# A one-core decoder layer: the queues of every engine but TensorE in another order, with each step naming its buffers

## The chip, the cores and the metric

One Trainium2 chip, one core. The metric is device microseconds of one execution of the whole kernel; lower is better. Engines are written as in the profile: PE (TensorE; PEld is its weight load), DVE (VectorE), ACT (ScalarE), POOL (GpSimd) and SP (SyncE, which here does nothing but issue DMAs).

## The reference, cut to what matters

The layer is computed in float32 on 512 positions of 1024 channels (depth 1).

```python
h   = rms_norm(x, attn_pre_norm)
mix = hybrid_mixer(h, ...)            # two head groups, one input and one output projection
x   = x + rms_norm(mix, attn_post_norm)
h   = rms_norm(x, ffn_pre_norm)
f   = (silu(h @ w_gate) * (h @ w_up)) @ w_down      # 1024 -> 2816 -> 1024
out = x + rms_norm(f, ffn_post_norm)
```

`hybrid_mixer` projects h, rotates queries and keys, and runs differential attention (4 heads: softmax of one map minus lambda times softmax of a second, values of 128) and native sparse attention (8 heads in 2 groups, with a compressed, a selected and a window branch, mixed by sigmoid gates). Both results are concatenated and multiplied by `w_out`.

## The kernel before

**Precision.** Every factor of a matmul is cut into a high part (ACT copies the float32 tile to fp32r) and a low part (DVE subtracts the high part from the tile), and a product is three matmuls: high by high, high by low, low by high. So nearly every weight tile costs one transfer, one ACT instruction and one DVE instruction of 512 or 1024 columns.

**The order is written by hand.** The kernel defines some 2600 named steps, each a function that issues a handful of instructions, and then calls them in the order of two long strings: `PLAN` (1387 steps: projection, attention, output projection) and `PLAN_NORM` with `PLAN_END` (1198 steps: norms and feed-forward). Nothing reorders behind that. Each engine takes its own instructions in the order in which the steps were called, and waits for data or a buffer where it must. So the place of a step among the steps of the same engine is that engine's queue, and the place among steps of other engines matters only through tiles: a tile is granted when its step is called. `at(t, fn, ...)` also notes a time for each step of the second half (`todo`), which orders only steps that stand in neither string.

**Stages.** To about 90 us the input projection runs: `xL`/`xH`/`xl` load and cut the eight tiles of x, `bL`/`bh`/`bl` and `fL`/`fh`/`fl` the weights, `F6.0` and the like are the matmuls. Up to about 230 us come the heads, `D0` to `D3` and `N0` to `N7`: `S` scores on PE, `X` the row maximum on DVE (L1051), `E` the exponential on ACT (L1055), `M` scaling on POOL (L1224), `T` transposes on PE, `H` and `L` the high and low parts (L1082 on ACT, L1085 on DVE), `V` the product with the values. `D0OH` is the high part of a finished head, `W2b` a quarter of the cutting of an output weight (POOL). Then the output projection and the norms.

**Feed-forward, up.** For each of 22 slices f of 128 columns, `load_ff` brings the gate and up weights, `sum_ff` (DVE) forms the sums of a Strassen-like scheme, `high_ff` (L1568) and `low_ff` (L1576) cut them, and seven steps `block.f.n` of 12 matmuls each (L1591) accumulate into a pair of PSUM banks (`yz`, and `x`). `snap_1` and `snap_2` (ACT) copy out of PSUM, `sum_x` (L1610) and `sums` (L1626, DVE) add, `gate_x` and `gate_c` (ACT) apply SiLU, `mult` (L1632, DVE) gives the activations. `block.f.4` comes after `sums.f` has read the bank it adds to.

**Feed-forward, down, first half.** The slices go in nine pairs p, again with seven products in place of eight. For pair p: `load_d.2p` brings a 1024-column tile of w_down into one of the three buffers `raw` (512 KB; L421), `load_22.p` half a tile into another (256 KB; L1676). `sums_a.p.0` (L1682) forms the other half of that buffer in place, `sums_a.p.1` (L1688) overwrites half of the first one, `sums_a.p.2` writes a third sum. `right_a.p.n.0` and `.1` (ACT, then DVE at L1708) cut the sums, `left_a.p.n.0` and `.1` (L1699 on DVE) the activations, `high_d` (L1714) and `low_d` (L1720) the tile. Once `low_d.2p` has run, the buffer of `load_d.2p` is free, and once `right_a.p.1.1` has run, that of `load_22.p`. `product_a.p.n` is six matmuls (L1665) into accumulators n = 5, 6, 7, 1. `pair_sums` forms sums of activations and sends two of them to DRAM; `load_b` and `load_s4` (L1756) bring them back into one of 36 slots of the pool S.

**Down, second half and end.** `sums_b`, `cut_b` (ACT, DVE) and `product_b` are the same for the other products; `down` (L1814) adds the last four slices directly, and `last_sum` (L1836), `last_square`, `last_mean`, `last_root`, `last_gain` (L1867) and `last_row` form the norm and the residual.

**Buffers.** A PSUM bank (8 of them), the weight buffers `raw`, `hi`, `lo` (three each) and the heads' tiles are taken in turn: the next tile gets the next buffer, in order of calls. Slots of S and the 20 wide slots of A are looked up in tables by the tile's name (`S_HOMES`, `HOMES`).

```python
n = taken[name] = taken.get(name, -1) + 1
return pool_.tile([P, w], dt, tag=homes[name][n], name=name, bufs=1)
```

Of the kernel before, what the change touches and what calls it, by code (L numbers as in the profile page):

```python
# [61 lines left out]
v0d2 fR10 F11.0 F11.1 pW0 Kh11 D0LD1 KX11 F11.2 F12.0 KX00 Kl11 Kp11 D0S10 D0S11 fR11 D0S12 D0Q12 v0d1 pA5 pH5 D0Q11
pL5 D0X12 KW12 Kh12 Kl12 D0X13 D0Q10 F12.1 F12.2 fL13 fh13 F13.0 fl13 F13.1 F13.2 KW13 Kh13 fR12 D0LD0 Kl13 KX12
Kp12 fL14 D0S00 KX13 Kp13 fR13 fh14 D0S01 KW00 fl14 pA6 D0E13 F14.0 F14.1 Kh00 F14.2 Kl00 fL6 fh6 D0X10 KX01 D0X11
pW5 pH6 D0E12 KW01 Kh01 F6.0 fl6 pL6 D0E11 v0a0 Kl01 D0E10 D0R Kp00 Kp01 KX03 K21 fR14 fL15 fh15 fl15 KW02 Kh02 Kl02
F6.1 pW6 KX02 KO1 F15.0 N0LD F6.2 fR6 KW03 Kh03 Kl03 fL7 F15.1 F15.2 fR15 pA7 N0K1 fh7 Kp02 Kp03 N0S11 D0S02 KO0 KT0
# [15 lines left out]
N2E10 N0V12 N2X11 N2Q12 N2Q11 N2R0 N2X12 N2g0 N2M01 D1T1 D1H1 D1L1 N0O1 N2M02 N2E12 N3Q0 N3X00 N2X13 W6b N2E11 D0RB
N2E13 D0ML D1V0 D1V1 D1V2 N0O2 N1T01 N2M03 N1H01 N2M00 N1T02 N1H02 N1L01 D1SQ N3SC N3CX N1TC N1HC N1T11 N2R1 N2g1
N2M13 N1L02 N1T12 N1H12 N3S01 N3S02 N1L12 D2S02 N3S1 N1H11 N1L11 N1T00 N3Q02 D1O3 N3Q01 N1H00 N2CM D2Q02 D2X03 N3E00
N3Q1 N3X01 N3X10 D2E03 N2M12 N1T10 N3X02 N2PH N3CA v1p3.0 N2PL N3E01 N3X03 D2S01 N1L00 v1p3.1 D2LD1 N2M11 D2S11
N1H10 N3E03 N1V00 N1VC N1L10 N3CE N3E02 N3CS N3R0 N3g0 N3CM D2S00 N3M02 N1V01 N1V02 N3M00 D2Q01 N3X11 D0OH D0OL v1a3
# [2060 lines left out]
```

## Time and profile before

| | us |
|---|---|
| median of 3 runs | 622.45 (621.71 to 622.87) |
| profiled execution | 622.45, span 620.5 |
| PE busy | 607.1 (98%) |
| PEld busy | 549.9 (89%) |
| DVE busy | 546.4 (88%) |
| ACT busy | 373.9 (60%) |
| POOL busy | 101.4 (16%) |
| DMA | 98.41 MB, 159 GB/s in the mean |

The granted TensorE clock of the profiled execution is 0.994 of full speed in the mean. The span is what the profile covers; the time beside it includes 1.95 us around it. A busy share is a mean over stages in which different engines are full: whether an engine matters at one point is seen only there, in the waits of PE, in the chain of work that ended last, and in the busy times of a stretch. An instruction's row gives its start, its duration, the line, the tile written and the tiles read.

### The profile page before, as it was taken

How to read it: one execution, taken by the hardware profiler on the slowest of the kernel's cores; microseconds unless marked ns; L12 is line 12 of the kernel's file. 1: busy time of each engine (PE TensorE's matmuls, PEld its weight loads, DVE VectorE, ACT ScalarE, POOL GpSimd, SP SyncE). 2: the span in 40 equal slices, each digit the busy share in tenths (PEclk: the TensorE clock that was granted, in tenths of full speed). 3: DMA queues.
4: the chain of work that ended last, by engine and by line, in shares of the span. 5: the costliest groups of instructions: out<-in, count | busy, mean ns of one | idle time of the engine just before them, and what ended most of it. 6: DMA issues, size and time to landing. Idle time of an engine off the chain costs nothing. (4 is left out here: it accounts for less than half of the span.)

```text
span 620.5 us, 10992 instructions
## 1 busy us (share of the span) xinstructions
PE 607.1 (98%) x4065; PEld 549.9 (89%) x4065; DVE 546.4 (88%) x965; ACT 373.9 (60%) x784; POOL 101.4 (16%) x153
## 2 busy tenths in 40 slices
PE   9999999999999999999999999999999799999995
PEld 5888888899999988889999999999999788878884
DVE  5898898997898884999999998899999699899977
ACT  6445375467999986577584565446464365577522
POOL 0030000307868878100000000000000000000000
PEclk9999999999999999999999999999999989999998
DMA  8566986646233211545143434353531554677413
GB/s 263 187 224 248 299 296 230 216 146 248 101 119 101 88 34 63 182 165 203 59 146 104 156 117 136 119 178 121 175 102 54 174 165 140 201 222 252 135 41 130
DMA packets 38341, 98.41 MB, mean 159 GB/s; under 512 B 4240, under 2 KB 11792, under 8 KB 37392
## 3 DMA queue, kind: packets, MB, share of 16 engines
q1 hardware_dynamic: 38144, 97.59, 47.3%
q8 instruction: 32, 0.52, 0.3%
q14 instruction: 21, 0.17, 0.1%
q10 hardware_dynamic: 144, 0.13, 0.1%
HBM read 82.10 MB, written 15.60 MB: 157 GB/s over the span
## 5 line engine op out<-in xcount | busy, mean ns | idle before, releaser
L1867 POOL TENSOR_TENSOR uf<-c,gain 128x512 f32<-128x512 f32 x1 | 1.3, 1277 | 360.1 <-DVE c L1836 360.1
L1055 ACT ACTIVATE p<-sc,nm 128x512 f32<-128x512 f32 (+3 forms) x96 | 50.2, 530 | 14.4 <-DVE nm L1051 12.9
L1051 DVE TENSOR_REDUCE nm<-sc 128x1 f32<-128x384 f32 (+3 forms) x96 | 43.4, 483 | 8.6 <-PE sc L1047 5.5
L1591 PE MATMUL yz<-rope,wbh 128*128 128x256 f32 x352 | 48.0, 280 | 0.0
L1224 POOL TENSOR_TENSOR p<-p,l 128x256 f32<-128x256 f32 (+3 forms) x64 | 45.3, 732 | 1.0
L1591 PEld LDWEIGHTS yz<-rope,wbh 128*128 128x128 f32 x352 | 44.1, 191 | 0.1
L1085 DVE TENSOR_TENSOR ptl<-tr,pth 128x384 fp32r<-128x384 f32 (+1 forms) x60 | 34.3, 592 | 8.4 <-ACT pth L1082 8.4
L1082 ACT ACTIVATE pth<-tr 128x384 fp32r<-128x384 f32 (+1 forms) x60 | 29.9, 530 | 7.3 <-PE tr L1072 6.8
L1568 ACT ACTIVATE whi<-wraw 128x1024 fp32r<-128x1024 f32 x22 | 23.2, 1057 | 13.3 <-DMA wraw<-in_wg 12.5
L1568 ACT ACTIVATE wbh<-wraw 128x1024 fp32r<-128x1024 f32 x22 | 23.3, 1057 | 12.6 <-DVE wraw L1555 7.7
L1576 DVE TENSOR_TENSOR wel<-e,weh 128x1024 fp32r<-128x1024 f32 x22 | 26.7, 1219 | 3.9 <-ACT weh L1568 2.6
L1568 ACT ACTIVATE weh<-e 128x1024 fp32r<-128x1024 f32 x22 | 23.2, 1056 | 8.0 <-DVE e L1550 6.9
L1072 PE MATMUL tr<-ident,p 128*128 128x128 f32 x200 | 27.8, 274 | 0.0
L1714 ACT ACTIVATE whi<-wraw 128x1024 fp32r<-128x1024 f32 x20 | 21.0, 1057 | 10.9 <-PE acc L1665 5.7
L1591 PE MATMUL yz<-rope,wbl 128*128 128x256 f32 x176 | 27.2, 276 | 0.0
L1576 DVE TENSOR_TENSOR wlo<-wraw,whi 128x1024 fp32r<-128x1024 f32 x22 | 26.8, 1217 | 0.0
L1576 DVE TENSOR_TENSOR wbl<-wraw,wbh 128x1024 fp32r<-128x1024 f32 x22 | 26.7, 1217 | 0.0
L1720 DVE TENSOR_TENSOR wlo<-wraw,whi 128x1024 fp32r<-128x1024 f32 x20 | 24.1, 1218 | 1.1 <-ACT whi L1714 1.1
L1621 ACT ACTIVATE us<-yz 128x512 f32<-128x512 f32 x22 | 13.0, 592 | 18.7 <-PE yz L1591 15.7
L1591 PEld LDWEIGHTS yz<-rope,wbl 128*128 128x128 f32 x176 | 23.4, 188 | 0.0
L1041 PE MATMUL sc<-kst,qst 128*128 128x384 f32 (+3 forms) x64 | 23.0, 367 | 0.3 <-DMA kst<-qk 0.3
L1072 PEld LDWEIGHTS tr<-ident,p 128*128 128x128 f32 x200 | 22.4, 141 | 0.7
(382 smaller groups left out, 1993.9 us busy)
## 6 DMA issues: line engine op xcount, KB each, us to landing
wraw<-in_wg SPq DMA_DIRECT2D x24, 512.0 KB, 3.7
wraw<-in_wu SPq DMA_DIRECT2D x22, 512.0 KB, 3.4
wraw<-in_wd SPq DMA_DIRECT2D x22, 512.0 KB, 3.7
qk<-rope SPq DMA_DIRECT2D x7, 1024.0 KB, 5.9
kst<-qk SPq DMA_DIRECT2D x24, 256.0 KB, 4.2
wraw<-in_wf SPq DMA_DIRECT2D x10, 512.0 KB, 4.2
wraw<-in_wo SPq DMA_DIRECT2D x8, 512.0 KB, 4.4
qst<-qk SPq DMA_DIRECT2D x16, 256.0 KB, 2.7
```

The lines of the kernel that those rows point to most:

```text
L1041: pe.matmul(sv[i], lhs, kk[:, 0, :w], start=(n == 0), stop=False, skip_group_check=True)
L1051: dve.tensor_reduce(nm[i], sv[i], AX.X, OP.max, negate=True)
L1055: act.activation(pp[i], sv[i], AF.Exp, bias=nm[i], accum_out=hs["l"][:, row, i:i + 1])
L1072: pe.transpose(tr[:, n * P:(n + 1) * P], pp[i][:, j * P:(j + 1) * P], ident)
L1082: act.activation(part(u, 0), tv[u], AF.Copy)
L1085: dve.tensor_tensor(part(u, 1), tv[u], f32(part(u, 0)), OP.subtract)
L1224: pool.tensor_tensor(p, p, hs["l"][:, 1 + br, i:i + 1].to_broadcast(list(p.shape)), OP.mult)
L1568: act.activation(t[0], w[src], AF.Copy)
L1576: dve.tensor_tensor(t[1], W[f][PARTS[n][0]], f32(t[0]), OP.subtract)
L1591: pe.matmul(o, W[f][w][wi][:, k * P:(k + 1) * P], hop[h][hi][:, k * HS:(k + 1) * HS], start=(n < 3 and m == 0), stop=(m == 11), skip_group ...
L1714: act.activation(hi, oa[f]["raw"], AF.Copy)
L1720: dve.tensor_tensor(lo, o["raw"], f32(o["w"][0]), OP.subtract)
```

## The change

Three things are done.

1. The steps of `PLAN` and `PLAN_NORM` stand in another order. The 800 steps of PE have the order that they had; those of SP, ACT, DVE and POOL are placed anew among them and among themselves, in all stages.
2. A step now names the buffers of the tiles that it creates, behind a colon, one character for each: `load_d.2:0` takes buffer 0 of `raw`, `sums.20:v` slot v of S. Every pool is laid out at the start, one buffer to a name, and `Spots` gives out what the step names. The names written are those of the buffers that the tiles had, so each tile keeps its address.
3. The tables of slots (`HOMES`, `S_HOMES`, `PLACES`, `S_PLACES`), `PLAN_END` and the times of `todo` go, since the plan now lists all steps. `run` calls them.

No instruction is added, removed or resized.

```diff
+class Spots:
+    def __init__(self, pool, tags, turn):
+        self.pool, self.tags, self.turn = pool, tags, turn
...
+    def tile(self, shape, dt, tag=None, name=None, bufs=1):
+        if tag in self.tags:
+            return self.pool.tile(shape, dt, tag=f"{tag}.{next(self.turn[0])}", name=name, bufs=1)
+        return self.pool.tile(shape, dt, name=name, bufs=bufs, **({"tag": tag} if tag else {}))
...
-    wpool = ctx.enter_context(tc.tile_pool(name="weights", bufs=3))
+    turn = [None]
+    wpool = Spots(ctx.enter_context(tc.tile_pool(name="weights", bufs=1)), ("raw", "hi", "lo"), turn)
+    for tag in ("raw", "hi", "lo"):
+        wpool.first(tag, "012", [P, 1024])
...
+    def run(plan):
+        for step in plan:
+            name, _, spots = step.partition(":")
+            turn[0] = iter(spots)
+            ops[name]()
+            assert not list(turn[0]), step
...
-    for tok in plan:
-        ops[tok]()
+    run(plan)
```

The plan itself is the bulk of the diff. The beginning, a stretch of the heads, and three stretches of the feed-forward, old and new:

```diff
-wu xL1 gc bL1.0 xH1 xl1 bL1.1 bh1.0 F0.0.1 bl1.0 F0.1.1 F0.2.1 bh1.1 bl1.1 F2.0.1 bL1.2 bh1.2 F2.1.1 bl1.2 F2.2.1
+wu:00 xL1:0 gc bL1.0:0 bh1.0:0 bl1.0:0 xH1:k bL1.1 bh1.1 xl1:e F0.0.1:7 bL1.2 F0.1.1 F0.2.1 bl1.1 bL2.0:2 F2.0.1:6
...
-D1T2 D1T0 D1H0 N1PL N1M13 N2S12 N0VC N0V10 N3S0 D1H2 N0V11 N1M11 N0L12 N2E01 N2CS N2S11 N2X10 N1M03 D1L0 D1L2 N1M10
...
+D1V2 N2X13:7 N1M12 N1M01 N2E12:1 N1M11 N2E01:0 D0ML N1T01:5 N2E13:3 N1H01:00 N2R0 N1T02:6 W3c:u W3d:t N1M13 N3SC:2 N1PL
...
+N3S02:2 D2S02:4 N1M00 N1H11 N2g0 D1O3:0 N2M01 N2M11 N2M00 N3S1:6 N1T00:3 N3X00:1 D0OH:dh N3X10:0 N3Q02 LW4:2 N2M03 N3Q01
+N2CM N1H00 N1L11 D2Q02 D2X03:2 N3Q1 N2PH:0 N1T10:7 v1p3.0:1 D2E03:2 N3X11:3 N2M13 N1H10 N3E10:0 D2LD1:0 D2S01:4 N3X03:6
...
-low_ff.15.b sums.12 low_ff.16.a low_ff.13.d gate_c.10 block.16.1 snap_1.16 block.16.2 low_ff.16.e block.16.5
...
+gate_x.12 sum_ff.16.1:b high_ff.15.b:ac low_ff.11.d low_ff.16.a sum_ff.16.2 block.10.4 gate_c.10 low_ff.15.b block.15.6
...
-sums_a.0.2 block.19.7 sums.19 block.20.2 block.21.6 sums.17 block.17.4 right_a.0.1.1 high_d.0 low_d.0 pair_sums.7.1
-pair_sums.6.3 load_s4.1 left_a.0.0.0 load_22.1 left_a.0.0.1 right_a.0.0.0 left_a.2.0.0 pair_sums.7.2 snap_2.21
-block.20.6 high_ff.21.b low_ff.21.b block.19.2 high_ff.19.d low_ff.19.d load_d.2 sums_a.1.0 pair_sums.6.4
...
-right_a.1.1.0 right_a.1.1.1 sums_a.1.2 high_d.2 low_ff.21.d low_d.2 high_ff.18.d sums.18 low_ff.18.d block.19.4
-block.21.7 load_22.2 load_d.6 sums_a.2.0 right_a.2.1.0 gate_c.19 block.21.3 sums.21 sums_a.2.1 block.20.3 sums_a.2.2
-left_a.6.0.0 right_a.2.1.1 block.18.4 gate_c.18 block.20.7 product_a.0.5 block.21.4 low_ff.20.d sums.20 block.20.4
...
+sums.19:q block.17.4 sums_a.0.1 pair_sums.7.1:d block.20.6 high_d.0:1 sums_a.0.2:2 right_a.0.1.0:ea gate_x.18 low_d.0:0
+high_ff.21.b:gi load_d.2:0 block.19.2:5 left_a.0.0.0:h9 right_a.0.1.1 pair_sums.4.3 high_ff.19.d:ut low_ff.21.b
+gate_c.17 block.20.5 low_ff.19.d left_a.0.0.1 pair_sums.7.2 block.21.2:3 load_22.1:1 pair_sums.6.4:x pair_sums.7.4
+mult.17 left_a.0.1.0 left_a.6.0.0:85 low_ff.21.d sums_a.1.0 snap_2.21:n sums_a.1.1 sums_a.1.2 block.19.4 snap_2.20:4
+right_a.1.1.0:db right_a.1.1.1 sums.18:0 load_d.4:2 block.21.7 left_a.0.1.1 high_d.2:2 sum_x.20:x low_d.2:1 load_22.2:1
+gate_c.19:5 block.21.3 high_ff.20.d:st high_ff.18.d:yv low_ff.18.d sums_a.2.0 left_a.2.0.0 low_ff.20.d right_a.2.1.0:1i
+load_s4.1:w sums_a.2.1 block.20.3 right_a.2.1.1 load_b.1:u sums_a.2.2:g sums.21:2 block.18.4 block.20.7 sums.20:v
...
-left_a.4.1.1 product_a.4.5 left_a.5.0.1 load_d.12 load_22.6 low_d.10 product_a.5.5 left_a.5.1.0 product_a.4.1
-left_a.5.1.1 product_a.5.1 sums_a.6.0 sums_a.6.1 sums_a.6.2 product_a.4.7 product_a.5.7 right_a.6.1.0 load_d.14
...
-left_a.7.1.1 gate_x.18 product_a.6.1 mult.18 gate_x.19 load_b.7 left_a.7.0.1 cut_act.18.0 left_a.8.1.1 product_a.6.7
...
-product_a.8.7 load_kept.3 low_d.16 product_a.8.1 load_d.1 cut_act.18.1 left_a.8.0.0 left_a.8.0.1 product_a.8.5
...
+sums_a.5.2 product_a.2.6 left_a.4.1.1 right_a.5.1.0:bd load_s4.0:f right_a.4.0.1 load_s4.2:7 load_d.12:2 cut_b.1.1.0:3
+low_d.10:2 left_a.5.0.1 right_a.5.1.1 load_22.6:0 left_a.5.1.1 product_a.3.6 left_a.7.1.0:i1 product_a.4.6 product_a.4.5
+load_b.5:y sums_a.6.0 product_a.5.5 product_a.4.1 left_a.8.1.0:06 load_d.14:1 sums_a.6.1 product_a.5.1 cut_b.2.2.0:9
...
+high_d.14:2 product_a.6.5 load_b.7:s right_a.6.0.1 left_a.8.1.1 cut_b.1.1.1 low_d.14:1 mult.19 load_d.3:0 load_d.16:2
+product_a.6.1 cut_act.18.0:g cut_b.3.1.1 left_a.7.0.0 load_22.8:1 left_a.8.0.0 left_a.7.1.1 sums_b.1 product_a.6.7
+product_a.6.6 left_a.7.0.1 cut_b.0.2.0:m high_d.3:0 cut_b.2.2.1 load_b.2:e low_d.3:2 right_a.7.0.0 sums_a.8.0 sums_a.8.1
...
+cut_b.0.2.1 right_a.7.0.1 product_a.7.5 product_a.7.7 load_d.1:0 product_a.8.7 low_d.16:0 gate_x.20 product_a.8.1
```

In the tail, `last_gain.0.0` stands ahead of `last_sum.0.1` instead of behind it.

More of the change, by code (lines that the diff above doesn't have):

```diff
@@ L62 @@
[L62 to L66, printed above, removed]
@@ L82 @@
[L82 to L86, printed above, removed]
@@ L182 @@
-pair_sums.7.4 gate_c.17 gate_x.17 mult.17 block.20.5 snap_2.20 high_ff.20.d block.21.2 sums_a.1.1 sum_x.20 load_d.4
-right_a.1.1.0 right_a.1.1.1 sums_a.1.2 high_d.2 low_ff.21.d low_d.2 high_ff.18.d sums.18 low_ff.18.d block.19.4
-block.21.7 load_22.2 load_d.6 sums_a.2.0 right_a.2.1.0 gate_c.19 block.21.3 sums.21 sums_a.2.1 block.20.3 sums_a.2.2
-left_a.6.0.0 right_a.2.1.1 block.18.4 gate_c.18 block.20.7 product_a.0.5 block.21.4 low_ff.20.d sums.20 block.20.4
-left_a.0.1.0 high_d.4 low_d.4 load_22.3 gate_c.21 cut_b.3.2.0 left_a.5.0.0 left_a.0.1.1 product_a.0.7 left_a.2.1.1
@@ L187 @@
-pair_sums.8.1 pair_sums.8.3 sum_x.21 sums_a.3.0 left_a.1.1.0 left_a.1.1.1 product_a.0.1 product_a.1.1 load_b.1
-left_a.4.1.0 load_b.3 product_a.1.7 product_a.2.7 sums_a.3.1 high_d.6 gate_c.20 pair_sums.8.2 load_s4.3 left_a.2.0.1
-load_s4.2 left_a.1.0.0 product_a.2.1 load_d.8 sums_a.3.2 right_a.3.0.0 low_d.6 right_a.1.0.0 cut_b.7.2.0
-right_a.0.0.1 right_a.3.1.0 right_a.3.0.1 pair_sums.7.3 right_a.3.1.1 left_a.3.1.0 left_a.1.0.1 sum_x.19
-right_a.1.0.1 load_22.4 sums_a.4.0 product_a.0.6 product_a.1.6 left_a.3.0.0 left_a.3.0.1 sums_a.4.1 sums_a.4.2
@@ L192 @@
-pair_sums.5.3 right_a.4.1.0 right_a.4.1.1 product_a.1.5 gate_x.20 product_a.2.5 product_a.3.5 load_d.10
-right_a.2.0.0 left_a.3.1.1 product_a.3.7 load_b.4 left_a.4.0.0 left_a.4.0.1 high_d.8 product_a.3.1 low_d.8
-cut_b.1.1.0 right_a.4.0.0 right_a.2.0.1 load_22.5 sums_a.5.0 right_a.5.1.0 sums_a.5.1 product_a.2.6 product_a.3.6
-high_d.10 right_a.4.0.1 product_a.4.6 sums_a.5.2 right_a.5.0.0 left_a.8.1.0 right_a.5.1.1 load_b.5 left_a.7.1.0
-left_a.4.1.1 product_a.4.5 left_a.5.0.1 load_d.12 load_22.6 low_d.10 product_a.5.5 left_a.5.1.0 product_a.4.1
@@ L197 @@
-left_a.5.1.1 product_a.5.1 sums_a.6.0 sums_a.6.1 sums_a.6.2 product_a.4.7 product_a.5.7 right_a.6.1.0 load_d.14
-right_a.6.1.1 left_a.6.0.1 cut_b.5.1.0 high_d.12 low_d.12 load_s4.0 cut_b.0.2.0 cut_b.0.2.1 load_22.7 right_a.5.0.1
-sums_a.7.0 left_a.7.0.0 cut_b.4.2.0 sums_a.7.1 load_b.2 right_a.6.0.0 right_a.6.0.1 load_d.16 sums_a.7.2
-product_a.5.6 right_a.7.1.0 right_a.7.1.1 product_a.6.5 left_a.6.1.0 left_a.6.1.1 cut_b.2.2.0 high_d.14 low_d.14
-left_a.7.1.1 gate_x.18 product_a.6.1 mult.18 gate_x.19 load_b.7 left_a.7.0.1 cut_act.18.0 left_a.8.1.1 product_a.6.7
@@ new lines @@
+sum_ff.21.3 pair_sums.6.1:m left_a.2.1.0:f0 load_d.0:0 load_22.0:1 block.21.1:4 gate_x.15 low_ff.21.e mult.14 block.21.5
+gate_c.15 block.19.7 pair_sums.6.2 block.20.2:7 mult.15 gate_x.17 sums_a.0.0 snap_1.21:l block.21.6 snap_1.20:y
+sums.19:q block.17.4 sums_a.0.1 pair_sums.7.1:d block.20.6 high_d.0:1 sums_a.0.2:2 right_a.0.1.0:ea gate_x.18 low_d.0:0
+high_ff.21.b:gi load_d.2:0 block.19.2:5 left_a.0.0.0:h9 right_a.0.1.1 pair_sums.4.3 high_ff.19.d:ut low_ff.21.b
+gate_c.17 block.20.5 low_ff.19.d left_a.0.0.1 pair_sums.7.2 block.21.2:3 load_22.1:1 pair_sums.6.4:x pair_sums.7.4
@@ new lines @@
+block.20.4 gate_c.18 left_a.1.1.0:34 low_d.4:2 mult.18 gate_c.20 load_d.8:2 gate_c.21:r left_a.2.1.1 pair_sums.6.3
+product_a.0.7:60 sum_x.21 sums_a.3.0 product_a.0.1:43 left_a.1.1.1 sums_a.3.1 right_a.0.0.0 load_s4.3:z right_a.0.0.1
+high_d.6:1 right_a.2.0.0 product_a.1.1 product_a.1.7 left_a.2.0.1 low_d.6:0 left_a.1.0.0 sums_a.3.2 pair_sums.8.2
+right_a.1.0.0 product_a.2.7 left_a.1.0.1 product_a.2.1 left_a.4.1.0:74 right_a.1.0.1 right_a.3.0.0:cj product_a.0.6:15
+right_a.3.1.0 pair_sums.8.3 right_a.2.0.1 left_a.3.1.0:59 product_a.1.6 left_a.3.0.0 pair_sums.5.3 load_22.4:0
@@ new lines @@
+part_of_sum.1.0:k sums_b.0 load_d.9:2 high_d.5:1 pair_sums.8.4:3 mult.21 cut_b.1.2.1 low_d.1:1 sums_b.2 cut_act.18.1:o
+product_a.7.6 product_a.8.6 part_of_sum.5.1:d part_of_sum.5.0:i mult.20 cut_b.0.1.0:6 cut_b.2.1.1 low_d.5:0
+part_of_sum.7.1:f cut_b.2.0.0:a load_d.7:1 part_of_sum.1.1:w cut_b.0.0.0:d cut_b.0.0.1 cut_b.5.2.0:j product_b.0.5
+load_d.15:0 product_b.1.5 product_b.2.5 cut_b.0.1.1 cut_b.1.0.0:c product_b.0.1 load_b.8:3 cut_b.1.0.1 cut_b.2.0.1
+high_d.9:2 cut_b.5.1.1 load_s4.4:v part_of_sum.7.0:e product_b.1.1 cut_act.20.0:8 product_b.2.1 high_d.7:0 sums_b.3
@@ L2050, in hybrid_block_kernel @@
         at(t + 0.15, last_root, i)
[L2051 to L2055 removed]
+    plan = PLAN_NORM.split()
+    assert sorted(step.partition(":")[0] for step in plan) == sorted(ops)
+    run(plan)
 def _rope_tables():
```

528 lines of the change are left out of this document (197 added, 331 removed).

## The prediction

> **What bounds the kernel now.** I began with parts 1 and 2 of the page, to see which engine leaves room.
>
> ```profile
> span 620.5 us, 10992 instructions
> PE 607.1 (98%) x4065; PEld 549.9 (89%) x4065; DVE 546.4 (88%) x965; ACT 373.9 (60%) x784; POOL 101.4 (16%) x153
> PE   9999999999999999999999999999999799999995
> ```
>
> PE leaves 13.4 us of 620.5 unused, in two visible places: one slice at four fifths of the span, and the end. The change keeps PE's order, so it can win only what PE waits for, or spend more. The list of waits, restricted to PE, says what that is.
>
> ```profile
> PE yz L1591 <- DVE vs L1626: 3.4, 1, 3.4
> PE warm L543 <- DVE warm L540: 1.2, 1, 1.2
> PE yz L1591 <- DVE wlo L1576: 0.5, 1, 0.5
> PE fm L691 <- DVE wlo L684: 0.3, 1, 0.3
> ```
>
> One wait of 3.4 us stands out. Next the chain of work that ended last, around it: the start, the length, what.
>
> ```profile
> 482.58 5.57 DMA wraw<-in_wd
> ...
> 495.96 4.59 PE yz L1591 x24
> 500.55 1.40 PE acc L1665 x6
> 501.94 2.83 PE yz L1591 x24
> 504.77 40.14 PE acc L1665 x174
> ...
> 544.94 0.69 DVE t L1688
> 545.63 1.21 DVE tl L1708 x2
> ```
>
> Two readings. First, the 24 matmuls right behind the wait (block.18.4 and block.20.7) took 4.59 us, and 24 like them a little later 2.83: the wait costs 3.4 and 1.76 more. Second, at 544.9 the chain passes from PE to DVE and back: DVE has no slack there, which is where a gain made at 492 has to pass.
>
> The busy times by stretch bear both out (columns PE, PEld, DVE, ACT, POOL, granted clock, DMA).
>
> ```profile
> 0.00:10.00 10.00, 8.47 (x27) 4.50 (x27) 3.24 (x8) 5.24 (x8) 0.33 (x5) 1.00 0.72 218
> 500.58:547.98 47.40, 47.26 (x217) 38.70 (x216) 43.70 (x68) 28.30 (x51) 0.00 (x0) 1.00 0.57 179
> 150.00:205.00 55.00, 54.67 (x426) 51.28 (x423) 50.19 (x126) 49.65 (x155) 41.04 (x66) 1.00 0.35 112
> 496.00:500.55 4.55, 4.55 (x25) 4.55 (x26) 4.17 (x7) 3.17 (x6) 0.00 (x0) 0.62 0.35 115
> ```
>
> Behind the wait the granted clock averages 0.62: that is the 1.76. From 500.58 to 547.98 DVE works 43.70 of 47.40 us. In 150 to 205 PE, DVE and ACT are all above 90%.
>
> **The change part by part.** Counted from the two plans, the steps that change place in their queue are 146 of 215 on SP, 494 of 623 on ACT, 725 of 858 on DVE and 112 of 132 on POOL. No tile gets another buffer, no instruction is added. So every cost is a matter of what now stands ahead of what; I price the places where PE's waits are, or where a queue is full, and bound the rest.
>
> *The wait at 492.* The queue of SP shows its origin, by its waits and its issues.
>
> ```profile
> SPq L1756 <- PE yz L1591: 9.4, 1, 9.4
> ```
> ```profile
> 481.69 0.33 SPq L1756 DMA_DIRECT2D s4b<-s  x1
> 482.58 0.38 SPq L421 DMA_DIRECT2D wraw<-in_wd  x1
> ```
>
> load_s4.1 (L1756) holds SP for 9.4 us, and load_22.1 and then load_d.2 (482.58) queue behind it. load_d.2 lands 5.57 us after its issue, at 488.2, and DVE stands idle for it:
>
> ```profile
> 483.84 0.68 DVE L1576 TENSOR_TENSOR dl<-d,dh 128x512 fp32r<-128x512 f32 x1
> 488.25 0.69 DVE L1682 TENSOR_TENSOR wraw<-wraw 128x512 f32<-128x512 f32 x1 [3.73 <-DMA wraw<-in_wd]
> ...
> 491.85 0.43 DVE L1610 TENSOR_TENSOR act<-x,snap 128x256 f32<-128x256 f32 x1 [1.03 <-DMA s<-s]
> 492.19 0.68 DVE L1708 TENSOR_TENSOR tl<-wraw,th 128x512 fp32r<-128x512 f32 x1
> 492.79 0.69 DVE L1688 TENSOR_TENSOR t<-wraw 128x512 f32<-128x512 f32 x1
> 493.99 1.22 DVE L1720 TENSOR_TENSOR wlo<-wraw,whi 128x1024 fp32r<-128x1024 f32 x1
> 495.13 0.68 DVE L1626 TENSOR_TENSOR vs<-yz,us 128x512 f32<-128x512 f32 x1
> ```
>
> The starts give DVE's pace: 0.60 us for 512 columns (492.19 to 492.79), 1.14 for 1024 (493.99 to 495.13), 0.34 for 256 (491.85 to 492.19). The row at 495.13 is sums.18, for which PE waits. In the new plan load_s4.1 stands behind load_d.4 and load_22.2. load_d.2 then waits for low_d.0 alone, which gives back its buffer. Ahead of low_d.0, sums.17 has gone earlier and right_a.0.1.1 later, so its end is at most the 481.2 of now, and I take 480.9. With 5.57 us again load_d.2 lands at 486.5. sums_a.1.0, 1.1, 1.2, right_a.1.1.1 and sums.18 are 5 x 0.60, so PE has its data at 489.5 and wants it at 492.5. The wait goes: **-5.2 us** (3.4 + 1.76). What covers it is 3.0 us; a landing later than 489.5 would bring it back.
>
> *The DVE stretch behind it.* From sums_a.1.0 to sums.21 the new queue holds 15 instructions, 13 x 0.60 + 1.14 + 0.34 = 9.3 us, so sums.20 starts at 495.8 (500.58 before). From sums.20 to the end of low_d.16, DVE had 43.70 us of work and 3.70 idle. The new plan puts six more ahead of low_d.16: cut_b.1.1.1, cut_b.3.1.1 and mult.19 (0.60 each), cut_b.4.2.1, cut_b.2.2.1 and pair_sums.6.3 (0.34 each); left_a.0.1.1 (0.60) has left. Work: 43.70 + 2.82 - 0.60 = 45.9. The idle changes too, by the way three buffers are handed back: load_22.p is issued when right_a.(p-1).1.1 is done, and sums_a.p.0 waits for it.
>
> ```profile
> 523.22 0.68 DVE L1708 TENSOR_TENSOR tl<-wraw,th 128x512 fp32r<-128x512 f32 x1
> ...
> 526.83 0.69 DVE L1682 TENSOR_TENSOR wraw<-wraw 128x512 f32<-128x512 f32 x1
> ...
> 532.75 0.69 DVE L1682 TENSOR_TENSOR wraw<-wraw 128x512 f32<-128x512 f32 x1 [0.44 <-DMA wraw<-in_wd]
> ...
> 542.41 0.69 DVE L1682 TENSOR_TENSOR wraw<-wraw 128x512 f32<-128x512 f32 x1 [1.68 <-issue]
> ```
> ```profile
> wraw<-in_wd SPq DMA_DIRECT2D x9, 256.0 KB, 3.1
> ```
>
> Such a load takes 3.1 us. Before, 523.22 (right_a.5.1.1) to 526.83 (sums_a.6.0) held four instructions and no idle time. After, left_a.4.1.1, left_a.5.0.1, right_a.4.0.1 and low_d.10 stand ahead of right_a.5.1.1, and left_a.5.1.1 (0.60) alone covers the load: 2.5 idle. For p = 7 the cover is 0.60 + 0.60 + 0.34: 1.5 idle. For p = 8 it is 4.5: none. That is 4.0 in place of 0 + 0.44 + 1.68 = 2.1. Idle: 3.7 to 5.6, and I take 5.6, because these rows fix it. So low_d.16 ends at 495.8 + 45.9 + 5.6 = 547.3, where it ended at 547.98 before. The matmul that needs it (in product_a.8.1) started 0.40 behind it:
>
> ```profile
> 548.38 0.39 PE L1665 MATMUL acc<-wlo,sh 128*128 128x512 f32 x1
> ```
>
> PE would now be there 5.2 us earlier, at 543.2, and can start at 547.3 + 0.05 (PE had been busy up to then, so the 0.40 is not a hand-over that must be paid; I take the least). So PE waits about 4.1 us, and of the 5.2 about **1.0 is left**; with idle at 3.7 it is 2.9. I expect the wait in two pieces, first for left_a.7.1.1 (product_a.7.1), then for low_d.16 (product_a.8.1), each behind part of the added work: an estimate of about 2 each.
>
> *The small waits.* low_ff.16.a, the 0.5 us wait, goes four instructions up DVE's queue: -0.5. bl1.0, the 0.3 us wait, goes ahead of xl1: -0.3. Both reach the end only as far as DVE keeps pace, which it does where it waits for PE. The wait for the warm-up tile stays.
>
> *The attention stage, 150 to 205.* All three engines are full here, so any step put ahead of one that PE needs soon shows.
>
> ```profile
> 159.52 0.49 ACT L1055 ACTIVATE p<-sc,nm 128x256 f32<-128x256 f32 x1
> 159.97 0.39 ACT L1055 ACTIVATE p<-sc,nm 128x128 f32<-128x128 f32 x1
> ...
> 163.92 0.88 ACT L1082 ACTIVATE pth<-tr 128x384 fp32r<-128x384 f32 x2
> ```
>
> N2E01 (159.52, 0.45 to the next) now stands behind D1H1 and directly ahead of N2E13 and N1H01 (163.92), and D0OH, one more activation, comes up ahead of N1H00. The two are 0.45 and, by the rows from 128x256 to 128x384 x2, about 0.5. Bounds: 0, if PE's own queue covers both, and 2, if smaller swaps like them add as much again. I take the two alone: **+1.0**. POOL is 41.04 of 55 us busy; its largest move is W2b, whose output is used only in the output projection, behind all heads; that slack covers it, and I leave it at nothing.
>
> *The first 90 us.* D0E13 now stands behind fh6, an activation of 1024 columns, and F6.0 needs the bank that it frees. An activation of this form takes 1.06:
>
> ```profile
> L1568 ACT ACTIVATE whi<-wraw 128x1024 fp32r<-128x1024 f32 x22 | 23.2, 1057 | 13.3 <-DMA wraw<-in_wg 12.5
> ```
>
> Between 0 and 1.06: **+0.3**, nearer to nothing, as DVE sets most of that chain. From 250 to 480 PE waits nowhere but in the row above, and I found no step that moves past its user's slack: 0.
>
> *The tail.* DVE's chain ends the kernel.
>
> ```profile
> 607.69 0.69 DVE c L1836
> 608.37 1.20 DVE uf L1867 x2
> ```
>
> One of the two L1867 (last_gain.0.0) moves ahead of 607.69, and the mean behind them starts when ACT's square is done: **-0.3**.
>
> Sum: -1.0 - 0.5 - 0.3 + 1.0 + 0.3 - 0.3 = -0.8. The profiled execution took 622.45 us (span 620.5 and 1.95 around it), which is also the median: **621.6 us**.
>
> **A rule against the trace.** The rows: after 3.4 us without work the clock falls to 0.62 on average; after the 1.2 us for the warm-up tile it does not (1.00 over the first 10 us, which contain that wait). What happens between is not shown. The Trainium skill, TensorE: Matmul & The Clock Gate, "Part 1: The HAM clock gate", says that about 3.4 us of idleness halve the clock, and that as much work brings it back. This trace agrees with 3.4. By that rule the new wait of 4.1 us, which I expect in two pieces of about 2, would leave the clock alone, and the sum stays; in one piece it would add 1.76.
>
> **The rivals.** *Kept gain.* DVE's idle time falls as PE runs on, and the stretch absorbs the 2.2 us of work: then the whole 5.2 remains instead of 1.0, and the time is 617.4. For it: the 3.70 idle exceed 2.2. Against: the chain passes through DVE at 544.9 already.
>
> *Slower: the new wait halves the clock.* PE's wait at product_a.7.1 becomes one of 3.4 us or more, because left_a.7.1.1 comes later on DVE. It decides once DVE is 1.4 us later there than I count (a first piece of 3.4 in place of 2), for instance with 3.7 us per load, an assumption, in place of 3.1 at two or three of the returns. The price: 1.4 for the delay and 1.76 for the slow clock, of which the second piece hides about a third, 2.6 in all: 621.6 + 2.6 = 624.2. For it: three returns in a row add up on a full engine. Against: the DMA share is only 0.57.
>
> *No effect.* The wait at 492 goes, or stays in part because load_d.2 lands late, and the DVE stretch decides alone; with the attention stage at 2 the sum is +0.2: 622.6.
>
> **How the numbers follow.** Less than 0.2% (1.24 us) can't be told from no change. My forecast 0.42 (its own range 620 to 623: faster 0.15, same 0.24, slower 0.03), kept gain 0.25, slow clock 0.18, no effect 0.15 (same 0.09, faster and slower 0.03 each). Faster 0.43, same 0.33, slower 0.24. The range runs from the kept gain, with 0.4 for the small waits that it would also save, to the slow clock: 617.0 to 624.3.
>
> **What would show it.** After the change, in PE's waits: no 3.4 for vs L1626, no SP wait of 9.4 at L1756, and DVE idle before L1682 near 488 under 1 us. New waits of PE for DVE's sl L1699 and wlo L1720 between 535 and 550, about 4 us in sum, with DVE idle for wraw<-in_wd of 2.5 and 1.5 before. The clock at 1.00 all through says that the pieces are short. If PE has no wait between 535 and 550, my tally of DVE is wrong, and the time is near 617; if the stage 150 to 205 takes no longer than 55.0, the +1.0 is.

## The result, and the profile after

631.43 us median (631.21 to 631.97) against 622.45: the ratio is 1.0147, 95% interval 1.0129 to 1.0164. The change costs 9.0 us where 0.8 of gain was forecast, and the time lies outside the range. (Ratios and medians here and below leave out three disturbed executions of splice2, at 860 to 2145 us.) First the head of the page of the changed kernel, then the first rows of its waits restricted to PE.

```profile
span 629.6 us, 10992 instructions
PE 611.7 (97%) x4065; PEld 550.0 (87%) x4065; DVE 550.8 (87%) x965; ACT 374.2 (59%) x784; POOL 103.2 (16%) x153
```
```profile
PE acc L1548 <- DVE sl L1582: 2.7, 1, 2.7
PE trh L1397 <- DVE pre L1367: 1.3, 2, 0.9
PE warm L424 <- DVE warm L421: 1.2, 1, 1.2
PE yz L1474 <- ACT snap L1484: 0.9, 2, 0.5
PE acc L1548 <- DVE tl L1591: 0.9, 1, 0.9
PE sc L922 <- DVE dr L1032: 0.7, 1, 0.7
```

(Lines are those of the changed kernel, 119 less than before in the heads and 117 less behind them: L1582 is `left_a`, L1591 `right_a`, L1548 `product_a`. In the hybrids below a line stands up to 4 further down.) The wait for sums.18 is gone. Of the two waits forecast in the products the first is there, 2.7 for left_a.7.1.1; the second, for low_d.16, is not in the list, and one of 0.9 for right_a.5.0.1 (in product_a.5.6), which was not forecast, is. All rows of the list sum to about 10 us, where before they summed to 6, and DVE is busy 4.4 us longer with the same 965 instructions. Neither shows where 9 us went. PE's order is the same, so each matmul can be laid beside itself: by how much later it starts than in the kernel before.

| first matmul of | before, at | late after, us | stretch | forecast |
|---|---|---|---|---|
| D0MS (heads) | 146.61 | 0.0 | 0.0 | 0.0 |
| mx30 (norms begin) | 250.39 | +5.6 | **+5.6** | +1.0 |
| block.0.6 | 299.86 | +7.6 | **+2.0** | 0 |
| block.19.5 | 466.02 | +8.7 | +1.1 | -0.5 |
| block.21.4 | 501.78 | +3.5 | -5.2 | -5.2 |
| product_b.0.5 | 553.45 | +9.2 | **+5.7** | +4.2 |
| last matmul | | +9.2 | 0.0 | -0.3 |

The gain at 492 came as forecast; that it fits to the tenth is luck, since between the same two matmuls the hybrids below that have this order gain 4.9 to 5.7. Three stretches lost more: 4.6 in the heads, 2.0 in the norms, 1.5 in the products (and 1.6 in the slices). In the heads, the busy times by stretch, before and after, between the same two matmuls (columns as above):

```profile
146.61:209.95 63.34, 63.01 (x488) 59.04 (x488) 57.59 (x145) 55.86 (x176) 47.13 (x76) 1.00 0.36 116
```
```profile
146.61:215.24 68.63, 65.72 (x489) 59.24 (x489) 61.18 (x147) 56.73 (x180) 56.17 (x88) 1.00 0.41 135
```

DVE works 3.6 us more on two instructions more, and POOL 9.0 more on twelve. One of the DVE instructions, with what POOL does meanwhile, after:

```profile
210.39 1.33 DVE L1109 TENSOR_TENSOR pc<-pc,l 128x128 f32<-128x128 f32 x1
```
```profile
210.31 1.27 POOL L1195 TENSOR_TENSOR wl<-wraw,wh 128x512 fp32r<-128x512 f32 x1
```

and the same instruction before, with POOL idle between its rows:

```profile
208.19 0.28 DVE L1228 TENSOR_TENSOR pc<-pc,l 128x128 f32<-128x128 f32 x1
```
```profile
207.09 0.40 POOL L1224 TENSOR_TENSOR p<-p,l 128x128 f32<-128x128 f32 x1
209.24 0.20 POOL L1155 TENSOR_TENSOR dr<-dr 128x4 f32<-128x4 f32 x1 [1.74 <-ACT dr L1179]
```

This is N5CM, the scaling of the compressed scores. It takes 0.28 alone and 1.33 when it starts under a POOL instruction: it ends 0.14 behind POOL's (211.72 against 211.58), as if it had stood still until then. For all eight steps of this form the groups say the same (before, after):

```profile
L1228 DVE TENSOR_TENSOR pc<-pc,l 128x128 f32<-128x128 f32 x8 | 2.3, 291 | 0.3 <-POOL l L1220 0.3
```
```profile
L1109 DVE TENSOR_TENSOR pc<-pc,l 128x128 f32<-128x128 f32 x8 | 5.8, 726 | 0.0
```

I sorted, in both traces, the DVE instructions that start while POOL is inside one, by where their wide inputs lie: in SBUF, the memory of ordinary tiles, or in PSUM, into which matmuls accumulate. With both in SBUF, 19 of 32 took over 0.12 us longer than the median of the same form alone; the 13 others started at most 0.24 us ahead of the end of POOL's instruction. With one in SBUF and one in PSUM, 0 of 138 did, and with a single one 0 of 160. The instructions held up this way between 146 and 215 are N1CM, N2CM, N3CA, N3CM, D2MX2, D2MX1, D2MX0, N4CM and N5CM, 4.6 us together; before, there is none in this stretch. The Trainium skill, SBUF — State Buffer, "Who interferes with whom", says this: GpSimd shares a port pair with VectorE, a VectorE instruction with two SBUF inputs contends with a GpSimd instruction that reads SBUF, and the one that comes second blocks until the first is done. The traces agree: 19 of 32 against 0 of 298.

### The profile page after: what moved, and what is told of

Its sections match the earlier page's. It is cut to its first block, busy times and chain, and to the rows that moved or that the text cites. A ratio compares the mean times of both kernels' runs of the same rounds, so it can differ in the third digit from the quotient of the medians.

```text
span 629.6 us, 10992 instructions
## 1 busy us (share of the span) xinstructions
PE 611.7 (97%) x4065; PEld 550.0 (87%) x4065; DVE 550.8 (87%) x965; ACT 374.2 (59%) x784; POOL 103.2 (16%) x153
## 4 chain that ended last, share of the span: by engine, by line
PE 39%; DVE 8%; DMA 2%; issue 1%; ACT 1%; DVEq 0%; SPq 0%; ACTq 0%
PE yz L1474 25%; PE acc L1548 8%; PE x L1474 3%; PE acc L1697 3%; DMA wraw<-in_wd 2%; DVE tl L1591 1%; DVE sl L1582 1%; DVE wraw L1565 1%; DVE wraw L1567 1%; DVE wlo L1603 1%; DVE c L1719 0%; DVE t L1571 0%; DVE uf L1754 0%; ACT uj L1734 0%; DVE e L1431 0%
## 5 line engine op out<-in xcount | busy, mean ns | idle before, releaser
L936 ACT ACTIVATE p<-sc,nm 128x256 f32<-128x256 f32 (+3 forms) x96 | 50.1, 528 | 15.4 <-DVE nm L932 14.2
L932 DVE TENSOR_REDUCE nm<-sc 128x1 f32<-128x128 f32 (+3 forms) x96 | 43.5, 480 | 7.6 <-PE sc L928 5.7
L1484 ACT ACTIVATE snap<-yz 128x256 f32<-128x256 f32 x22 | 8.2, 378 | 25.6 <-PE yz L1474 22.7
```

The source lines that it names most:

```text
L932: dve.tensor_reduce(nm[i], sv[i], AX.X, OP.max, negate=True)
L936: act.activation(pp[i], sv[i], AF.Exp, bias=nm[i], accum_out=hs["l"][:, row, i:i + 1])
```

## The experiments

All hybrids are the changed kernel with the strings of steps rearranged; each step keeps its buffers. "Late" below is the start of a matmul against the same one in the kernel before, in one profiled execution of each.

**Where it is: ctl, head_only, norm_only, b_s4.**

```diff
 ctl:       PLAN of before, PLAN_NORM of before, in the form with buffers named
 head_only: PLAN of after,  PLAN_NORM of before
 norm_only: PLAN of before, PLAN_NORM of after
 b_s4 (from ctl):
-pair_sums.6.3 load_s4.1 left_a.0.0.0 load_22.1 ... block.21.7 load_22.2
+pair_sums.6.3 left_a.0.0.0 load_22.1 ... block.21.7 load_22.2 load_s4.1:w
```

> The new way of naming buffers, with every step in the order of before. Theory 'order': each tile keeps its address and each queue its order, so this is the kernel before, 622.4 us within 0.2%. Rival 'naming': if handing out each buffer under a name of its own makes other waits, this run shows part or all of the 9.0 us, up to 631.

> The new order in PLAN (projection, attention, output projection), the order of before in PLAN_NORM. Theory 'two places that add': PE is 5.3 to 5.7 us late where the norms begin (matmul at 285.93 before, 291.59 after), so 622.4 + 5.5 = 627.9. Rival 'the seam': the loss in the norms (2.6 us between 293 and 308 after the change) comes from what the heads leave behind, and then it is here too: 630.5.

> The order of before in PLAN, the new order in PLAN_NORM (norms and feed-forward). Theory 'two places that add': what is left of the 9.0 us, 3.4, so 625.9: +3.4 from the norms to 480, -5.3 at the wait for sums.18, +5.7 at product_a.5.6 and 7.1. Rival 'the seam': the norms lose nothing of themselves, 623.3. My prediction's own sum for this part was -2.1 to -1.5: 620.6.

> The order of before in all but one step: load_s4.1 stands behind load_22.2, so that load_22.1 and load_d.2 no longer queue behind it. Theory 'one step makes the gain': the wait for sums.18 goes and 5.2 us with it, and as no work is added ahead of low_d.16, DVE gives back only what it lacks: low_d.16 stays at 547.98 minus the 3.7 us of idle time at most; I expect 618 to 620.5. Rival 'DVE decides': DVE's work from sums.20 to low_d.16 fills the stretch and all is given back: 622.4.

ctl: 622.95, ratio 1.0002 (0.9983 to 1.0021): naming the buffers costs nothing that this interval would show, and what is left is the order. head_only: 628.91, 1.0096 (1.0076 to 1.0115), and PE loses 5.6 between D0MS and mx30, as in the table. norm_only: 626.62, 1.0063 (1.0042 to 1.0085). The two add to 10.3 against 9.0, about what such runs scatter by, and the loss in the norms appears without the new heads (1.8 between mx30 and block.0.6; in head_only 0.7). b_s4: 619.91, 0.9957 (0.9942 to 0.9972): one step moved makes the old plan 2.7 us faster, inside its range, and its clock stays at 1.00 there. Of the old plan's wait of 3.4, 1.6 is left, now for DVE's own queue:

```profile
PE yz L1475 <- DVE vs L1510: 1.6, 1, 1.6
```

**The heads: apart, collide.** Only DVE steps with two inputs in SBUF are moved, POOL's work is untouched.

```diff
 apart (from head_only), places within DVE's queue:
+D2MX2 -1, D2MX0 +1, D2MX3 +3, N5CM -3, N4CM -5, D1MX2 -6
 collide (from ctl):
+N5CA +3, N4CA +1, D3MX2 +2, D3MX1 -2, N2CM -2, D1MX2 +3, D0MX3 -8
```

> As head_only (628.9), with six DVE steps moved within DVE's queue: D2MX2 one place up, D2MX0 one down, D2MX3 three down, N5CM three up, N4CM five up, D1MX2 six up. All have two inputs in SBUF; in head_only five of them ran while POOL was in an instruction and took longer than alone: D2MX2 0.34 us, D2MX1 0.77, D2MX0 0.39, N4CM 0.17, N5CM 0.91, 2.6 in all. Theory 'POOL holds them up': with POOL's work and its order as they are, the steps fall into POOL's pauses, and 2 to 4 us are won: 625 to 627. Rival 'the order of DVE and ACT': what PE waits for comes later because other steps stand ahead of it; six short steps moved by a few places leave that as it is: 628.4 to 629.4.

> As ctl (the order of before, 622.9), with seven of DVE's steps with two inputs in SBUF moved by at most eight places within DVE's queue, so that they come up while POOL is in an instruction: N5CA three down, N4CA one down, D3MX2 two down, D3MX1 two up, N2CM two up, D1MX2 three down, D0MX3 eight up. No other step moves. Theory 'POOL holds them up': each that meets a POOL instruction costs 0.2 to 0.9 us on a full DVE: 625 to 628, with these steps' rows longer by the same sum. Rival 'the order': 622.5 to 623.5, as the steps are 0.3 to 0.6 us long and their users are not near.

apart: 628.08, 1.0103 (1.0074 to 1.0132), which misses its range. The moved steps partly met other POOL instructions, and N5CA and D2MX3 were held up in place of those freed: 3.0 us of holding up in the stretch in place of 4.0, and PE loses 4.1 from D0MS to N5T11 (a matmul at 209.95 before) in place of 5.3. The medians differ by 0.8 only, inside the scatter: inconclusive by its time.

collide: 630.20, 1.0115 (1.0073 to 1.0157): above its range of 625 to 628, 7 us lost by moving seven short steps by at most eight places. The worst one, with POOL's instruction:

```profile
204.98 1.59 DVE L1095 TENSOR_TENSOR pc<-pc,nmc 128x128 f32<-128x128 f32 x1
```
```profile
204.05 2.38 POOL L1247 TENSOR_TENSOR wlo<-wraw,whi 128x1024 fp32r<-128x1024 f32 x1
```

In ctl no instruction of this form took over 0.30. The held-up time is about 7.2 us in all against 2.5 in ctl, so nearly 5 of the 7 are held-up time; the rest comes with it, in part as a slow clock, which ctl does not have there:

```profile
148.77:215.66 66.89, 65.23 (x488) 60.58 (x489) 59.56 (x145) 56.75 (x178) 48.73 (x79) 0.97 0.34 111
```

**The heads, with the second input taken away: ctl_free, head_free.**

```diff
+    def alone(tile_):
+        dve.tensor_reduce(tile_, tile_.unsqueeze(2), AX.X, OP.add)
...
-            dve.scalar_tensor_tensor(pp[0][i], pp[1][i], hs["l"][:, 1, i:i + 1], pp[0][i], OP.mult, OP.add)
+            alone(pp[0][i])
...
-            dve.tensor_tensor(cv, cv, hs["l"][:, 0].unsqueeze(2).to_broadcast([P, NT, NPAD]), OP.mult)
+            alone(cv.rearrange("p i n -> p (i n)"))
```

> As ctl, with the 24 steps NxCM and DxMX replaced by a tensor_reduce over a row of one: it has the same tile as output and one input in SBUF in place of two; the scaling by the reciprocal sum and the difference of the two maps are left out. The control for head_free: here only one of these steps (D0MX2, 0.16 us) was held up. Both theories: 622 to 622.9.

> As head_only, with the same replacement: the order of all steps stays, the 24 steps no longer have a second input in SBUF, and the scaling and the difference are left out. Theory 'POOL holds them up': the seven of these steps that were held up between 146 and 215 lose 3.2 us (0.27, 0.34, 0.34, 0.77, 0.39, 0.17, 0.91); N3CA (0.78) keeps its two inputs and stays late. 625 to 626. Rival 'the order of DVE and ACT': the order is the same, 628 to 629.

Both kernels leave out the scaling of the compressed scores and the difference of the two maps, so they serve to measure and do not compute the layer. ctl_free: 622.05, 0.9995 (0.9980 to 1.0010). head_free: 626.53, 1.0060 (1.0041 to 1.0078), 2.4 faster than head_only and 0.5 above its range of 625 to 626. The order of every step is the same in both. The stretch shows it without the scatter of the rest (head_only, head_free):

```profile
146.76:215.41 68.65, 65.89 (x489) 59.15 (x489) 60.73 (x147) 56.78 (x180) 56.31 (x88) 1.00 0.40 135
```
```profile
146.71:212.73 66.02, 65.09 (x490) 59.25 (x489) 57.22 (x147) 56.66 (x180) 54.53 (x88) 1.00 0.42 140
```

DVE has 3.5 us less work in the same 147 instructions, and the stretch is 2.6 shorter. The 13 replaced steps in it take 3.8 us less: 0.6 because the reduce is the shorter form (as between ctl and ctl_free), 3.2 because they are no longer held up. In ctl_free the stretch is as long as in ctl (63.4), so the shorter form wins nothing in the old order. The replaced step also no longer waits for the reciprocal and the second map, which ctl_free shows to be worth nothing where nothing is held up; that it is worth nothing under the new order is not shown. Of the 5.3 lost up to N5T11, 2.6 thus go with the second input, POOL's but for what the shorter form and the dropped waits may be worth here; 2.7 remain, of which N3CA (0.87) and N4CA (0.18), which kept their two inputs, are held up still. The last 1.6 I put to the order itself; no run shows that by itself, nor the two ACT steps that the forecast priced.

**The products: na_six, na_ret.**

```diff
 na_six (from norm_only), DVE steps moved from ahead of low_d.16:
+right_a.8.0.1 cut_b.2.2.1 cut_b.1.1.1 cut_b.4.2.1 mult.19 cut_b.3.1.1
 na_ret (from norm_only):
+right_a.5.1.0:bd right_a.5.1.1 load_s4.0:f right_a.4.0.1 ...
+sums_a.6.1 right_a.6.1.0:fc ... sums_a.6.2:j right_a.6.1.1 left_a.6.0.1 ... low_d.12:0
```

> As norm_only (626.6), with five of the DVE steps that the change put ahead of low_d.16 (cut_b.2.2.1, cut_b.1.1.1, cut_b.4.2.1, mult.19, cut_b.3.1.1, 2.5 us) moved behind right_a.8.0.1. Theory 'the work ahead' (the term +2.2 of the prediction): PE's wait of 2.9 for left_a.7.1.1 falls by 2.1 to 0.8, the clock stays full (1.3), and low_d.16 comes 2.5 earlier: 623.0 to 624. Rival 'work only put off': the next products wait for low_d.1 and low_d.5 instead: 625.5 to 627.

> As norm_only (626.6), with right_a.5.1.1 directly behind right_a.5.1.0 and right_a.6.1.0 and 6.1.1 ahead of left_a.6.0.1 and low_d.12, so that load_22.6 and load_22.7 are issued earlier and DVE has work while they run. Theory 'the way back of the buffers' (idle 2.6 and 2.0 us before sums_a.6.0 and 7.0): 2.3 + 1.7 of that goes, the waits at product_a.5.6, 7.1 and 8.1 (0.9, 2.7, 1.0) with them, and the clock stays full: 620.7 to 622. Rival 'the work ahead': DVE is full anyway, and the waits come back: 625.5 to 627.

First the stretch in the changed kernel, DVE's instructions behind three of the loads:

```profile
525.46 0.69 DVE L1565 TENSOR_TENSOR wraw<-wraw 128x512 f32<-128x512 f32 x1 [0.98 <-DMA wraw<-in_wd]
...
534.37 0.69 DVE L1565 TENSOR_TENSOR wraw<-wraw 128x512 f32<-128x512 f32 x1 [2.62 <-DMA wraw<-in_wd]
...
542.49 0.69 DVE L1565 TENSOR_TENSOR wraw<-wraw 128x512 f32<-128x512 f32 x1 [2.02 <-DMA wraw<-in_wd]
```

na_six, which moves five of the six steps: 627.74, 1.0092 (1.0070 to 1.0113): nothing won. PE's wait for left_a.7.1.1 shrank from 2.7 to 0.9, and the work came due at once: waits for low_d behind it rose from 1.0 to 2.7.

```profile
PE acc L1550 <- DVE wlo L1605: 2.7, 3, 1.2
...
PE acc L1550 <- DVE sl L1584: 1.3, 2, 0.9
```

na_ret: 622.30, 0.9998 (0.9986 to 1.0011): 4.3 won by letting three instructions go earlier. The idle times before the sums are now 0.90, 0.37 and 0.34 (the last two were 2.68 and 1.91 in norm_only), and of the three waits in the products one of 1.0 is left.

```profile
526.54 0.69 DVE L1567 TENSOR_TENSOR wraw<-wraw 128x512 f32<-128x512 f32 x1 [0.37 <-DMA wraw<-in_wd]
...
532.97 0.69 DVE L1567 TENSOR_TENSOR wraw<-wraw 128x512 f32<-128x512 f32 x1 [0.34 <-DMA wraw<-in_wd]
```

What cost was idle time, not work.

**The norms: norm_u, norm_v.** In norm_only DVE, from 252 on:

```profile
253.65 0.68 DVE L1440 TENSOR_TENSOR wraw<-wraw 128x512 f32<-128x512 f32 x1
255.46 1.23 DVE L1461 TENSOR_TENSOR wbl<-wraw,wbh 128x1024 fp32r<-128x1024 f32 x1 [1.13 <-ACT wbh L1453]
257.42 1.38 DVE L1329 TENSOR_TENSOR mixt<-mix,rope 128x512 f32<-128x512 f32 x2 [0.74 <-PE mix L1223]
```

These are U3.0, Vb.0 and mS0; Ve.0 and U4.0, for which all was there, stand behind them.

```diff
 norm_u (from norm_only): U3.0 directly behind U1.0, c2.s4 behind pr30
 norm_v (from norm_only):
-U1.0:3 mx20:60 U2.0 mx03 ... U3.0 ... Hb.0:bc Vb.0 mS0:f ... He.0:ae ... Ve.0 mx31 U4.0:d
+U1.0:3 U3.0 mx20:60 U2.0 U4.0:d mx03 ... Hb.0:bc He.0:ae Vb.0 Ve.0 mS0:f
```

> As norm_only (626.6), with two DVE steps moved: U3.0 directly behind U1.0 (as before the change) and c2.s4 behind pr30 (as before). Theory 'DVE's queue in the norms': in norm_only PE loses 1.8 us between mx30 and tr30 (waits of 0.5 and 0.9 for pr31 and pr30) and 0.4 more to block.0.6, since Vb.0 waits 1.2 us for a high part that ACT can form only after U3.0, and c2.s4 (0.6) stands ahead of pr30, on an engine without other idle time. Both moved: tr30 is at most 0.3 later than it was, 624.6 to 625.3. Rival 'POOL': U1.0 and the step behind it are held up by the last two POOL steps of the heads (1.0 us each) whichever step comes second; then the stretch stays late and 626 to 627 remains.

> As norm_only (626.6), with the steps that stood ahead of mS0 before the change put back there: U3.0 directly behind U1.0, U4.0 behind U2.0, He.0 (ACT) behind Hb.0 and Ve.0 behind Vb.0; c2.s4 stays ahead of pr30. In norm_only and in norm_u DVE stood idle for 1.9 us around 255 to 258 (1.13 before Vb.0 and 0.74 before mS0; in norm_u 0.53 and 1.32), waiting for Hb.0 and for PE's mx07, while Ve.0 and U4.0 (1.14 and 0.60) were queued behind mS0; before the change there was no such idle time, and from there to 300 DVE is full. Theory 'idle time that a full queue never makes up': with the work back ahead of mS0 the 1.8 us go, tr31 starts as it did before the change relative to mx30 (42.8 us behind it), and the time is 624.5 to 625.2. Rival 'c2.s4 and sum_ff.2.4 ahead of l3.s2': tr31 recovers, but block.0.6 stays 1.2 late: 625.8 to 626.3.

norm_u: 625.37, 1.0050 (1.0031 to 1.0068), just above the theory's range, but block.0.6 is 1.8 late against mx30, as in norm_only: both causes that I had named were wrong. norm_v: 624.80, 1.0034 (1.0016 to 1.0052), inside the range of its theory; the idle time is gone (mS0 starts at 257.04, directly behind Ve.0), tr31 is in time again, and block.0.6 is 1.0 late. So 0.8 of 1.8 was idle time that a nearly full DVE (44.2 of the 45.5 us from 257.4 on, in norm_only) did not make up, and 1.0 is left, as the rival had it; that it is c2.s4 and sum_ff.2.4 ahead of l3.s2 was not tried. (In the changed kernel POOL's last two steps of the heads hold up U1.0 and U2.0 by 1.0 each; before, only U3.0 was held up, by 1.1. What this costs was not tried either.)

**Versions that beat both: splice, splice2.**

```diff
 splice: order of before up to sums.19, from there that of na_ret
 splice2 (from splice): mult.19 behind low_d.11, cut_b.3.1.1 behind cut_b.0.1.1
```

> PLAN and PLAN_NORM in the order of before up to sums.19, from there the order of na_ret (steps that were done by then left out). If the places are independent, as the runs so far say: the wait for sums.18 and the slow clock behind it go (5.2), nothing is lost in heads, norms or the slices, and DVE has work while load_22.6 and load_22.7 run, so that little is given back: 622.5 - 5.2 - 0.3 = 617.0, between 616.3 and 618.5. If DVE's work in the stretch decides after all, as in b_s4: 619.5 to 620.5.

> As splice (618.2), whose last loss is PE's wait of 1.2 us in product_a.8.1 for low_d.16: mult.19 moves behind low_d.11 and cut_b.3.1.1 behind cut_b.0.1.1, 1.2 us of DVE work that nobody needs before. Theory 'the work ahead costs where it stands, if it can wait': 617.0, 616.5 to 617.5. Rival 'work only put off' (as in na_six): low_d.1, low_d.5 or a later cut comes late by as much: 618.0 to 618.5.

splice: 618.22, 0.9934 (0.9921 to 0.9948), 4.3 faster than before and inside its range. splice2: 0.9931 (0.9905 to 0.9957), profiled execution 618.01; the 616.5 to 617.5 forecast was missed, and its rival's 618.0 to 618.5 came. The wait for low_d.16 shrank from 1.0 to 0.7, which the times do not tell apart. PE's waits in splice2 are short:

```profile
PE warm L425 <- DVE warm L422: 1.2, 1, 1.2
PE yz L1475 <- DVE wlo L1460: 0.9, 2, 0.5
PE acc L1549 <- DVE wlo L1604: 0.7, 1, 0.7
```

## Why the prediction was wrong, step by step

**The wait at 492: right.** It goes, with the slow clock behind it: -5.2 between block.19.5 and block.21.4, as summed. b_s4 shows that one step, load_s4.1, made most of it: moving it alone gains 3.8 between the same matmuls.

**The products: the idle time right, its size off by 1.4, the clock's price wrong.** The forecast had low_d.16 end at 547.3 on a clock where nothing else moved; it ended at 557.39, and with the 8.7 that PE was late before the stretch that is 548.7, 1.4 later. Sums.20 came 0.6 late, and the idle time before sums_a.5.0 I had left as it was (0.35; now 0.98); the 2.62 and 2.02 I had at 2.5 and 1.5. Those 1.4 us on DVE are the whole of what is off in this stretch. The slower rival's mechanism came too: the wait at product_a.7.1 was 2.7 and not 2, and the clock fell.

```profile
550.04:552.20 2.16, 2.16 (x5) 1.77 (x6) 2.16 (x4) 0.54 (x2) 0.00 (x0) 0.50 0.42 148
```

But it cost next to nothing. In norm_only the same wait of 2.7 left the clock at 1.00:

```profile
545.60:547.76 2.16, 2.15 (x9) 1.80 (x10) 2.16 (x4) 0.50 (x2) 0.00 (x0) 1.00 0.49 150
```

There PE is early and waits 1.0 for low_d.16; in the changed kernel it is slow and does not wait. From block.21.4 to the matmul that needs low_d.16 norm_only and the changed kernel lose nearly the same, 5.4 and 5.6: DVE decides, and the second wait hides nearly all of the slow clock, not a third of it as the rival had it. (In norm_u the half clock behind the same wait lasted twice as long, and the loss was 6.7.)

I had used the rule of about 3.4 us that the prediction cites from the Trainium skill (TensorE: Matmul & The Clock Gate, "Part 1: The HAM clock gate") to hold a shorter piece harmless. Here 2.7 us without work halved the clock in one run and not in another; the measurement decides, and 3.4 is no safe bound. (The 1.2 us for the warm-up tile, which the prediction took as harmless, do not bear on it: that wait stands ahead of the first matmul, and the nine behind it, of 512 columns, start 0.43 apart, where matmuls of 512 columns from 6.10 on start 0.23 apart.) The step that failed is also how I split the give-back: I counted 2.2 us for the six steps put ahead of low_d.16. na_six moved five of them and won nothing, because the work is due soon anyhow, and na_ret shows that the ways back of the buffers cost 4.3.

**The heads: the step that failed most.** I bounded the attention stage by 0 and 2 from two ACT instructions, and left POOL "at nothing" because W2b has slack. That looked at when POOL's results are needed, and not at what POOL does to DVE while it works. Measured: 5.6. In it DVE instructions stand held up by POOL for 4.6; head_free frees 3.2 of the 4.0 in head_only and wins 2.6. The trace of before shows the effect in two rows of 0.68 alone: 1.78 at 115.72 (pA3, under POOL's 115.47 to 116.95), and POOL's L1278 (251.27 to 252.57) holding up U3.0:

```profile
251.34 1.77 DVE L1555 TENSOR_TENSOR wraw<-wraw 128x512 f32<-128x512 f32 x1
```

The old order has its compressed steps and differences in POOL's pauses, as while POOL waits for a reciprocal; a tally of queues sees no difference between that place and one three steps away. The upper bound of 2 was drawn from rows of the wrong engine, ACT.

**The norms and slices: forecast at nothing.** I looked for steps that had moved past their users' slack, step by step. Nothing there had: tr31's own inputs moved little. What moved was work out of an idle time at 255, and on an engine that is then nearly full for 45 us it was not made up: 0.8 of the loss. The cause of the other 1.0 stays open. The slices lost 1.1: PE falls back by 1.3 at two waits for ACT's snap (0.9 in sum) and wins 0.7 at low_ff.16.a, which went as forecast; the rest is small waits, and the snaps were not tried alone. ctl, with the old order, lost 1.2 in the same stretch, at other waits, so a loss of this size is inside what single executions scatter by.

**The small terms.** bl1.0 and the first 90 us: PE was 0.9 late at 30 us, and in time again at 146; such lags are absorbed where PE later waits for something else. The tail: 0.0, not -0.3.

The upper end of the range, 624.3, was the slow clock on top of +1.0 for the heads. No case had a term for POOL or for the norms, so none reached higher.

## What to carry to other kernels

When steps are moved on engines that share something, ask of each pair what runs beside what, not only what stands ahead of what: on a full DVE, a 0.3 us instruction with two SBUF inputs took up to 1.6 when it came up under a POOL instruction. On a full engine, price idle time first: find each place where it waits for a transfer or for another engine, and see which steps filled that place; taking work out of a full stretch won nothing here (na_six), while an unfilled wait was paid nearly in full in na_ret (3.9 us of idle time, 3.5 between block.21.4 and product_b.0.5) and less than half in norm_v (1.9 us, 0.8). A large reordering is best taken apart by stages with PE's order as the ruler: the one good move was worth 2.7 us alone (b_s4), and 4.3 with the new order behind it and its idle times filled (splice).

## What was not expected of the hardware

The same wait of PE did not always do the same to its clock. The wait of 2.7 us at product_a.7.1 was followed by 3.4 us at 0.50 in the changed kernel (549.6 to 553.0) and by 6.8 us in norm_u (544.1 to 550.9), while in norm_only and norm_v the clock stayed at 1.00. The wait of 3.4 us for sums.18 was followed by 3.4 us at 0.50 before (496.5 to 499.9) and by 6.8 in ctl (495.6 to 502.4), which has the same order. In collide the clock fell after waits of 0.54 and 0.83 us close together at 207 to 209: it was 0.76 from 208 to 213, while waits of 0.5 and 0.9 in the norms of the changed kernel and one of 1.2 in na_six (at 558.6) left it at 1.00. What decides stays open.
